# A hybrid trunk's FFN products in another order, its down contraction over both PSUM pools, and its last gate steps spread over a projection

## The chip, the core and the metric

The kernel runs on one core of one Trainium2 chip. The time is the device time of the whole program in microseconds (us), the median of several runs. Before the change it is 2257.92 us (three runs, 2255.95 to 2261.97).

The core has a matmul engine (PE, or TensorE), whose weight loads run beside its matmuls (PEld), a vector engine (DVE), an activation engine (ACT), GpSimd (POOL) and a sync engine (SP) that only issues transfers. Each engine runs its own queue of instructions in order and waits for the others by semaphores. Matmuls write to PSUM, eight banks of 128 x 512 float32; everything else lies in SBUF or in the chip's memory.

## The reference, cut to what matters

Two layers, 512 tokens, width 1024, FFN width 2816. Each layer is

```python
x = x + 0.5 * swiglu(rmsnorm(x, ffn1_norm[l]), ffn1_w_gate[l], ffn1_w_up[l], ffn1_w_down[l])
x = x + hybrid_mixer(rmsnorm(x, mix_norm[l]), w_in[l], w_out[l], ...)
x = x + 0.5 * swiglu(rmsnorm(x, ffn2_norm[l]), ffn2_w_gate[l], ffn2_w_up[l], ffn2_w_down[l])

def swiglu(h, wg, wu, wd):
    return (jax.nn.silu(h @ wg) * (h @ wu)) @ wd
```

The mixer projects its input once (`w_in`), runs an mLSTM, a Mamba-2 scan and a convolution module on the parts, and projects back (`w_out`). Two of those parts matter here: the gates (the columns `i_pre`, `f_pre` and `dt`, from which come cumulative sums, running maxima and exponentials) and `z`, a plain projection of 1024 columns under a SiLU.

## The kernel before, in words

**Precision.** A float32 product is made of three matmuls: each operand is split into a rounded high part and the rest (high x high, high x low, low x high). Weights arrive by DMA in tiles called `raw` (three buffers) or `half` (six buffers); `split_w` makes `whi` on ACT (L176) and then `wlo` on DVE (L177), each in three buffers, for 1024 columns' worth at a time. A split waits until one of its three buffers has been read for the last time by PE.

**The FFN.** There are four (two a layer), each of one block of 256 columns and five blocks of 512. A block of 512 (`gated`) computes gate and up columns together by seven products instead of eight, in the manner of Strassen and Winograd: tokens, input rows and (gate, up) columns are each cut in two. On the right stand sums of weight tiles, which a DMA with `accum_op=add`, issued by POOL (`plus`, L363), makes in place; on the left stand the normed input `xh`, `xl` (products "11", "12", "22") or combinations of its quarters `chi`, `clo` that `combine` has made (products "5", "6", "7", "3"). Each product is 24 matmuls of 128x512 in two halves of 12, each half with its own `split_w`. In the order of the text of before:

- "11" takes the gate tiles `g1` into PSUM tiles A; then `plus` adds an up tile to `g1`, while `u1` and `u2` are loaded and `plus` adds to `u1`
- "12" takes `g2` (a `raw` tile) into A; the gate's SiLU (L388) reads A
- "5" takes the changed `g1` into C; `plus` adds to `g1` again
- "6" takes that `g1` into B; `plus` adds a third time; L398 and L399 fold B and C into `u` and `w`
- "7" takes `u1` into E; L404 folds it into `w`
- "3" takes `u2` into C on top of "5"
- "22" takes the `g1` of three sums into E on top of "7"

Every use of `g1` but the first follows the landing of a `plus` transfer, which itself waits until the split of the use before has read `g1`. Then 16 transposes (L421) turn the result, and the block's down product (`contraction`, L190 to L192) adds it to the residual `xT` in eight tiles of 12 matmuls, which DVE evicts one by one (L328). The blocks overlap: block n+1's "11" runs before block n's contraction, so the order on PE is products of n, "11" of n+1, contraction of n, products of n+1. In the first FFN's first block, called the opening block below, `combine` runs on DVE and ACT at the same time, and its scratch takes four of the six `half` buffers.

**PSUM.** Two pools of four banks: `pacc` (A, C, E, projections, the contraction) and `pmix` (B, transposes, small things). A holds two `pacc` banks over the contraction, which goes round the other two.

**The mixer.** `gates` is a generator of six steps. Step 3 ends in a store of rows to memory (`ssd_rows`, L600), which POOL loads back (L720), masks (L721) and ACT exponentiates (L724). Step 4 transposes (L607, L608), takes running maxima on DVE (L609 to L618, one chunk after the other) and exponentials on ACT (L616 to L625). Step 5 transposes those (L629, L631). `weave` runs one step of one generator per step of another, so the program's text lays gate steps between the convolution and the SSD projections.

**Order.** The text order is not the order on the engines. Tile, the scheduling layer, places instructions by priority and its own cost model; `shifted(-SOON)` raises the priority of an eviction.

Of the kernel before, what the change touches and what calls it, by code (L numbers as in the profile page):

```python
# [8 lines left out]

# [2 lines left out]

# [13 lines left out]
P = 128  # L28
# [17 lines left out]
SOON = 200  # L46
# [3 lines left out]
def trunk(ctx: ExitStack, tc: tile.TileContext, I: dict, out: bass.AP):  # L50
# [26 lines left out]
    def pacc():  # L77
        return ps_p.tile([P, S], F32, tag="acc", name="pacc")
# [218 lines left out]
        for _ in contraction(acts, wrows, scale, nxt):  # L297
            pass

    def contraction(acts, wrows, scale, nxt):  # L300

        nk = len(acts)
        per = 2048 // nk // (2 * P) * 2 * P
        step = 1024 // nk // P * P
        for o in range(0, D, per):
            v = stream([w[:, o:o + per].rearrange("(k p) d -> p k d", p=P) for w in wrows], nk, per)
            for q in range(0, per, step):
                hv, lv = split_w(v[:, :, q:q + step])
                tiles = [[(hv[:, k, m * P:(m + 1) * P], lv[:, k, m * P:(m + 1) * P], *acts[k]) for k in range(nk)]
                         for m in range(step // P)]  # L310
                pss = []
                if o + q == 0:
                    pss = [pacc() for _ in tiles[0:2]]
                    for part in (slice(0, max(nk - 2, 1)), slice(max(nk - 2, 1), nk)):
                        for ps, terms in zip(pss, tiles):
                            mm3(ps, terms[part], part.start == 0, part.stop == nk)
                for m, terms in enumerate(tiles):
                    d = (o + q) // P + m
                    if m < len(pss):
                        ps = pss[m]  # L320
                    else:
                        ps = pacc()
                        mm3(ps, terms)
                    with shifted(-SOON):
                        if scale == 1.0:
                            nc.vector.tensor_tensor(xT[d], ps, xT[d], op=add)
                        else:
                            nc.vector.scalar_tensor_tensor(xT[d], ps, scale, xT[d], op0=mul, op1=add)  # L328
                    if nxt is not None:
                        nxt.prep(d)  # L330
                    if d % 2:
                        yield

    def gated(nrm, wg, wu, c0, acts):
# [5 lines left out]
        def product(left, right, ps, start=True):  # L340
            for _ in product_halves(left, right, ps, start):
                pass
# [38 lines left out]
            for t in two:  # L381
                nc.scalar.copy(u[t], A[t])
        yield
        product("12", g2, A, start=False)
        gate = [tmp() for _ in two]
        with shifted(-SOON):
            for t in two:
                nc.scalar.activation(gate[t], A[t], AF.Silu, scale=r[:, t:t + 1])  # L388
        C = [pacc() for _ in two]
        product("5", g1, C)  # L390
        plus(g1, du2)
        B = [pmix() for _ in two]
        product("6", g1, B)
        plus(g1, dg2)
        w = [tmp() for _ in two]
        with shifted(-SOON):
            for t in two:
                nc.vector.tensor_tensor(u[t], B[t], u[t], op=add)  # L398
                nc.vector.tensor_tensor(w[t], C[t], u[t], op=add)  # L399
        E = [pacc() for _ in two]  # L400
        product("7", u1, E)
        with shifted(-SOON):
            for t in two:
                nc.vector.tensor_tensor(w[t], E[t], w[t], op=add)  # L404
        product("3", u2, C, start=False)
        act = [tmp() for _ in two] + w
        with shifted(-SOON):
# [19 lines left out]
    def ffn(nrm, wg, wu, wd, nxt, side=iter(()), pair=None, ready=(), final=None):  # L427
# [7 lines left out]
        for gi in range(len(blocks) + 1):  # L435
# [36 lines left out]
            if last and final:  # L472
                final.finish(acts, wd[f0:f0 + len(acts) * P, :], sign)
            else:
                held = contraction(acts, [wd[f0:f0 + len(acts) * P, :]], sign, after)
                if gi == len(blocks) - 1 and not final:
                    next(held)
                    next(held)
# [15 lines left out]
    def mixer(l, nrm, par, nxt):  # L494
# [521 lines left out]
        weave(glu_pair(0, R), spread(gate, (0, 1, 0, 1)), 1)  # L1016
        with shifted(0):
            nrm.apply()
        weave(ssd_proj(0, G[0]), gate, 1)
        drain(z_proj(0))  # L1020
        weave(ssd_inner(0, G[0], Z[0], r01), ssd_proj(1, G[1]), 1)
        weave(ssd_inner(1, G[1], Z[0], r01), chain(glu_pair(1), ssd_proj(2, G[2]), z_proj(1)), 2)
        weave(ssd_inner(2, G[2], Z[1], r23),
# [235 lines left out]
```

## Time and profile before

| | |
|---|---|
| median of three runs | 2257.92 us |
| the profiled execution's own time | 2266.93 us |
| its span, first to last instruction | 2264.9 us |
| PE busy | 2229.0 us, 98% |
| PEld, DVE, ACT, POOL busy | 81%, 73%, 50%, 12% |
| mean granted clock of PE | 0.995 |
| read from memory | 304.65 MB, 135 GB/s |

The profile is of one execution, a little slower than the median run. "Busy" of PE is a sum over rows whose ends are modelled: matmuls overlap, a row lasts longer than the distance to the next start, so short delays between matmuls show no idle time. A row of the timeline gives start, length, engine, line, operation and the tiles (out<-in), then in brackets the idle time ahead of it and what ended it.

### The profile page before, as it was taken

How to read it: one execution, taken by the hardware profiler on the slowest of the kernel's cores; microseconds unless marked ns; L12 is line 12 of the kernel's file. 1: busy time of each engine (PE TensorE's matmuls, PEld its weight loads, DVE VectorE, ACT ScalarE, POOL GpSimd, SP SyncE). 2: the span in 40 equal slices, each digit the busy share in tenths (PEclk: the TensorE clock that was granted, in tenths of full speed). 3: DMA queues.
4: the chain of work that ended last, by engine and by line, in shares of the span. 5: the costliest groups of instructions: out<-in, count | busy, mean ns of one | idle time of the engine just before them, and what ended most of it. 6: DMA issues, size and time to landing. Idle time of an engine off the chain costs nothing.

```text
span 2264.9 us, 27297 instructions
## 1 busy us (share of the span) xinstructions
PE 2229.0 (98%) x10339; PEld 1836.5 (81%) x10339; DVE 1644.2 (73%) x2357; ACT 1126.9 (50%) x1633; POOL 274.5 (12%) x305
## 2 busy tenths in 40 slices
PE   8899999999999999999999999999999999999998
PEld 7688788788888878888887888877888888888887
DVE  6666567999966775666776666688999588666557
ACT  5443345767555543434443344466665555433334
POOL 0221110100100012111011111101101000211110
PEclk9999999999999999999999999999999999999999
DMA  6876653333332277677376777433323324867662
GB/s 200 211 186 159 158 113 95 113 94 93 107 106 72 84 198 175 171 177 175 91 185 168 168 185 168 94 96 94 111 81 108 100 68 145 201 162 167 150 155 66
DMA packets 189539, 308.62 MB, mean 136 GB/s; under 512 B 9144, under 2 KB 68952, under 8 KB 189408
## 3 DMA queue, kind: packets, MB, share of 16 engines
q1 hardware_dynamic: 139712, 208.68, 28.0%
q0 software_dynamic: 48608, 97.04, 24.3%
q8 instruction: 82, 1.34, 0.2%
q10 hardware_dynamic: 1088, 1.16, 0.1%
q14 instruction: 49, 0.40, 0.1%
HBM read 304.65 MB, written 2.19 MB: 135 GB/s over the span
## 4 chain that ended last, share of the span: by engine, by line
PE 82%; issue 6%; DMA 4%; DVE 4%; ACT 3%; POOL 1%; SPq 0%; POOLq 0%; ACTq 0%; DVEq 0%
PE pacc L191 13%; PE pacc L192 13%; PE pacc L190 13%; PE pacc L356 8%; PE pacc L357 8%; PE pacc L355 8%; DMA half<-in_ffn_w_up_dram 3%; PE pacc L880 2%; PE pacc L881 2%; PE pacc L882 2%; PE pmix L356 2%; PE pmix L357 1%; PE pmix L355 1%; DVE wlo L177 1%; PE pmix L421 1%
## 5 line engine op out<-in xcount | busy, mean ns | idle before, releaser
L176 ACT CAST whi<-raw 128x1024 fp32r<-128x1024 f32 (+1 forms) x276 | 285.8, 1037 | 415.1 <-PE pacc L191 314.0
L177 DVE TENSOR_TENSOR wlo<-half,whi 128x1024 fp32r<-128x1024 f32 x240 | 291.3, 1223 | 214.6 <-ACT whi L176 214.2
L176 ACT CAST whi<-half 128x1024 fp32r<-128x1024 f32 x240 | 250.3, 1052 | 386.2 <-PE pacc L357 162.6
L177 DVE TENSOR_TENSOR wlo<-raw,whi 128x1024 fp32r<-128x1024 f32 (+1 forms) x276 | 332.8, 1208 | 109.4 <-ACT whi L176 108.3
L190 PE MATMUL pacc<-atile,whi 128*128 128x512 f32 x928 | 361.6, 392 | 1.4 <-DVE xT L328 1.4
L191 PE MATMUL pacc<-atile,whi 128*128 128x512 f32 x928 | 362.1, 390 | 0.3
L192 PE MATMUL pacc<-atile,wlo 128*128 128x512 f32 x928 | 361.9, 390 | 0.0
L363 POOL DMA_DIRECT2D half<-in_ffn_w_up_dram x120 | 144.4, 1239 | 1077.0 <-DVE wlo L177 700.5
L328 DVE SCALAR_TENSOR_TENSOR xT<-pacc,xT 128x512 f32<-128x512 f32 x184 | 126.7, 691 | 174.8 <-PE pacc L192 174.7
L190 PE MATMUL pacc<-xh,whi 128*128 128x512 f32 x608 | 242.7, 400 | 0.0
L192 PE MATMUL pacc<-xh,wlo 128*128 128x512 f32 x608 | 237.9, 392 | 0.0
L191 PE MATMUL pacc<-xl,whi 128*128 128x512 f32 x608 | 237.7, 392 | 0.0
L190 PEld LDWEIGHTS pacc<-atile,whi 128*128 128x128 f32 x928 | 174.0, 188 | 39.0 <-DVE xT L328 3.0
L191 PEld LDWEIGHTS pacc<-atile,whi 128*128 128x128 f32 x928 | 174.2, 188 | 37.2 <-DVE atile L183 1.6
L192 PEld LDWEIGHTS pacc<-atile,wlo 128*128 128x128 f32 x928 | 174.4, 188 | 36.1
L355 PE MATMUL pacc<-whi,chi 128*128 128x512 f32 x480 | 187.4, 391 | 3.6 <-ACT whi L176 2.5
L356 PE MATMUL pacc<-wlo,chi 128*128 128x512 f32 x480 | 187.6, 391 | 0.5 <-DVE wlo L177 0.5
L355 PE MATMUL pacc<-whi,xh 128*128 128x512 f32 x480 | 188.1, 392 | 0.0
L357 PE MATMUL pacc<-whi,clo 128*128 128x512 f32 x480 | 187.4, 391 | 0.0
L356 PE MATMUL pacc<-wlo,xh 128*128 128x512 f32 x480 | 187.2, 390 | 0.0
L357 PE MATMUL pacc<-whi,xl 128*128 128x512 f32 x480 | 187.2, 390 | 0.0
L693 DVE SCALAR_TENSOR_TENSOR cacc<-upad,pA,cacc 128x512 f32<-128x512 f32 x240 | 175.8, 766 | 1.1
(330 smaller groups left out, 3727.0 us busy)
## 6 DMA issues: line engine op xcount, KB each, us to landing
half<-in_ffn_w_up_dram POOLq DMA_DIRECT2D x120, 512.0 KB, 7.0
raw<-in_ffn_w_down_dram SPq DMA_DIRECT2D x44, 1024.0 KB, 5.1
half<-in_ffn_w_up_dram SPq DMA_DIRECT2D x80, 512.0 KB, 4.6
raw<-in_w_in_dram SPq DMA_DIRECT2D x40, 1024.0 KB, 5.4
raw<-in_ffn_w_gate_dram SPq DMA_DIRECT2D x23, 1024.0 KB, 5.2
half<-in_ffn_w_gate_dram SPq DMA_DIRECT2D x40, 512.0 KB, 7.0
half<-in_ffn_w_gate_dram POOLq DMA_DIRECT2D x40, 512.0 KB, 6.0
raw<-in_w_out_dram SPq DMA_DIRECT2D x10, 1024.0 KB, 4.9
```

What stands on the lines that cost most here:

```text
L176: nc.scalar.copy(hv, v)
L177: nc.vector.tensor_tensor(lv, v, hv.bitcast(F32), op=sub)
L190: nc.tensor.matmul(ps, wh, ah, start=start and k == 0, stop=False)
L191: nc.tensor.matmul(ps, wh, al, start=False, stop=False)
L192: nc.tensor.matmul(ps, wl, ah, start=False, stop=stop and k == n - 1)
L328: nc.vector.scalar_tensor_tensor(xT[d], ps, scale, xT[d], op0=mul, op1=add)
L355: nc.tensor.matmul(ps[t], ah, hv[:, i, :], start=start and k == 0, stop=False, **more)
L356: nc.tensor.matmul(ps[t], ah, lv[:, i, :], start=False, stop=False, **more)
L357: nc.tensor.matmul(ps[t], al, hv[:, i, :], start=False, stop=k == 3, **more)
L363: nc.gpsimd.dma_start(v, b[:, 2 * j:2 * j + 2, :], accum_op=add)
L693: nc.vector.scalar_tensor_tensor(o, u[:, j:j + S], col(cA, j * 4 + c), o, op0=mul, op1=add)
L880: nc.tensor.matmul(pv[c], xh[k][:, cs(c)], hv[:, k2, :], start=k == 0, stop=False)
```

## The change

It does three things. In `gated` the order becomes "11", "5", "7", "6", "12", "3", "22"; E moves to `pmix`, so that all four `pmix` banks and four `pacc` banks are held in a block, and the three evictions into `u` and `w` come in one group. `contraction` takes its tiles' banks in turn from a list of pools, for the FFN `pacc` and `pmix`, elsewhere `pacc` alone. In the mixer, z's projection follows the first SSD projection in one chain, and the gate's last three steps are laid at the first, third and sixth step of that chain.

```diff
-    def contraction(acts, wrows, scale, nxt):
-
+    def contraction(acts, wrows, scale, nxt, banks=(pacc,)):
+
+        turn = cycle(banks)
+        bank = lambda: next(turn)()
...
-                    pss = [pacc() for _ in tiles[0:2]]
+                    pss = [bank() for _ in tiles[0:2]]
...
-                        ps = pacc()
+                        ps = bank()
...
-        product("12", g2, A, start=False)
-        gate = [tmp() for _ in two]
-        with shifted(-SOON):
-            for t in two:
-                nc.scalar.activation(gate[t], A[t], AF.Silu, scale=r[:, t:t + 1])
         C = [pacc() for _ in two]
         product("5", g1, C)
         plus(g1, du2)
+        E = [pmix() for _ in two]
+        product("7", u1, E)
         B = [pmix() for _ in two]
         product("6", g1, B)
         plus(g1, dg2)
...
                 nc.vector.tensor_tensor(u[t], B[t], u[t], op=add)
                 nc.vector.tensor_tensor(w[t], C[t], u[t], op=add)
-        E = [pacc() for _ in two]
-        product("7", u1, E)
+                nc.vector.tensor_tensor(w[t], E[t], w[t], op=add)
+        product("12", g2, A, start=False)
+        gate = [tmp() for _ in two]
         with shifted(-SOON):
             for t in two:
-                nc.vector.tensor_tensor(w[t], E[t], w[t], op=add)
+                nc.scalar.activation(gate[t], A[t], AF.Silu, scale=r[:, t:t + 1])
         product("3", u2, C, start=False)
...
-                held = contraction(acts, [wd[f0:f0 + len(acts) * P, :]], sign, after)
+                held = contraction(acts, [wd[f0:f0 + len(acts) * P, :]], sign, after, (pacc, pmix))
...
-        weave(ssd_proj(0, G[0]), gate, 1)
-        drain(z_proj(0))
+        weave(chain(ssd_proj(0, G[0]), z_proj(0)), spread(gate, (1, 0, 1, 0, 0, 1)), 1)
+        drain(gate)
```

The matmuls are the same in number and size; what moves is their order. Three places show it.

**Place one, a regular block (the first FFN's second block).** On ACT the splits name the tile that they read: `raw_859` is "12"'s `g2`, `half_797` and `half_799` are `g1`, `half_875` and `half_877` are `u1`, `half_881` and `half_883` are `u2`. Before:

```order
L176 CAST whi_1033<-raw_859 128x1024
L176 CAST whi_1037<-raw_859 128x1024
L176 CAST whi_1071<-half_797 128x1024
L176 CAST whi_1075<-half_799 128x1024
L388 ACTIVATE tmp_1065<-pacc_801,nr_321 128x512
L388 ACTIVATE tmp_1066<-pacc_802,nr_321 128x512
L176 CAST whi_1107<-half_797 128x1024
L176 CAST whi_1111<-half_799 128x1024
L176 CAST whi_1149<-half_875 128x1024
L176 CAST whi_1153<-half_877 128x1024
```

After:

```order
L176 CAST whi_1035<-half_797 128x1024
L176 CAST whi_1039<-half_799 128x1024
L176 CAST whi_1071<-half_875 128x1024
L176 CAST whi_1075<-half_877 128x1024
L176 CAST whi_1105<-half_797 128x1024
L176 CAST whi_1109<-half_799 128x1024
L176 CAST whi_1147<-raw_859 128x1024
L176 CAST whi_1151<-raw_859 128x1024
```

Two splits of `u1` now stand between the two uses of `g1`, and those of `g2` after both. On DVE, behind the same block's "6", the evictions now stand in one group ahead of the low split of "3" (`half_881`). After:

```order
L177 TENSOR_TENSOR wlo_1152<-raw_859,whi_1151 128x1024
L397 TENSOR_TENSOR u_885<-pmix_1103,u_885 128x512
L397 TENSOR_TENSOR u_886<-pmix_1104,u_886 128x512
L398 TENSOR_TENSOR tmp_1139<-pacc_1033,u_885 128x512
L398 TENSOR_TENSOR tmp_1140<-pacc_1034,u_886 128x512
L399 TENSOR_TENSOR tmp_1139<-pmix_1069,tmp_1139 128x512
L399 TENSOR_TENSOR tmp_1140<-pmix_1070,tmp_1140 128x512
L177 TENSOR_TENSOR wlo_1184<-half_881,whi_1183 128x1024
```

Before, four evictions (there L398 and L399) stood ahead of that split and the two of E (there L404) behind the next.

**Place two, the first layer's gates.** On ACT, L724 exponentiates a mask row loaded back from memory (`rb`), L616 to L625 are the gates' exponentials, `raw_3366` and `raw_3424` hold z's weights. Before:

```order
L647 ACTIVATE mtile_3191<-mtile_3191 128x512
L724 ACT_TABLE_LOAD
L724 ACTIVATE rb_3490<-rb_3490,nlc_2860 128x128
L647 ACT_TABLE_LOAD
L647 ACTIVATE mtile_3232<-mtile_3232 128x512
L616 ACT_TABLE_LOAD
L616 ACTIVATE atile_3241<-atile_3240,mc_2868 4x128 x2
L620 ACTIVATE mc_2868<-mc_2868 4x1
L176 CAST whi_3396<-raw_3366 128x1024
L616 ACTIVATE atile_3241<-atile_3240,mc_2868 4x128
L620 ACTIVATE mc_2868<-mc_2868 4x1
L625 ACTIVATE atile_3238<-atile_3238,mc_2868 4x128 x3
```

After:

```order
L176 CAST whi_3382<-raw_3352 128x1024
L644 ACTIVATE mtile_3269<-pacc_3244,pC_1811,pB_1351 128x512
L647 ACTIVATE mtile_3232<-mtile_3232 128x512
L724 ACT_TABLE_LOAD
L724 ACTIVATE rb_3490<-rb_3490,nlc_2860 128x128 x4
L724 ACTIVATE rb_3499<-rb_3499,nlc_2860 128x128 x4
L647 ACT_TABLE_LOAD
L647 ACTIVATE mtile_3269<-mtile_3269 128x512
L616 ACT_TABLE_LOAD
L616 ACTIVATE atile_3278<-atile_3277,mc_2868 4x128 x2
L176 CAST whi_3426<-raw_3424 128x1024
L620 ACTIVATE mc_2868<-mc_2868 4x1
```

Eight mask exponentials instead of one now stand ahead of the first L616, and z's second split (`whi_3382` after, `whi_3396` before) ahead of them. On PE, the transposes of step 5 (L629, L631) among z's matmuls (L880 to L882), before:

```order
L882 MATMUL pacc_3363<-whi_3368,xl0_100 128x512
L629 MATMUL pmix_3313<-ident_75,atile_3238 128x4
L880 MATMUL pacc_3362<-whi_3368,xh1_93 128x512
L629 MATMUL pmix_3313<-ident_75,atile_3238 128x4
L881 MATMUL pacc_3362<-wlo_3369,xh1_93 128x512
L882 MATMUL pacc_3362<-whi_3368,xl1_101 128x512
L629 MATMUL pmix_3313<-ident_75,atile_3238 128x4
```

After:

```order
L880 MATMUL pacc_3350<-whi_3382,xh3_95 128x512
L881 MATMUL pacc_3350<-wlo_3383,xh3_95 128x512
L882 MATMUL pacc_3350<-whi_3382,xl3_103 128x512
L629 MATMUL pmix_3410<-ident_75,atile_3275 128x4 x3
L631 MATMUL pmix_3410<-ident_75,atile_3276 128x4 x4
L880 MATMUL pacc_3348<-whi_3426,xh4_96 128x512
```

The transposes now stand together. Between the last transpose of step 4 (L608) and the first L629 stood 51 matmuls of 128x512 (45 of a projection, 6 of z) and now stand 60 (24 and 36); L607 itself stands 21 matmuls later. On DVE the low split of z's second tile now stands ahead of L609, and that of its third tile ahead of L621. The same holds in the second layer.

**Place three, the opening block on POOL.** `half_387` and `half_389` are `g1`, `half_481` and `half_483` are `u1`. Before:

```order
L363 DMA half_387<-in_ffn1_w_up_dram 128x2x512
L363 DMA half_389<-in_ffn1_w_up_dram 128x2x512
L363 DMA half_387<-in_ffn1_w_gate_dram 128x2x512
L363 DMA half_481<-in_ffn1_w_up_dram 128x2x512
L363 DMA half_483<-in_ffn1_w_up_dram 128x2x512
L363 DMA half_389<-in_ffn1_w_gate_dram 128x2x512
```

After:

```order
L365 DMA half_387<-in_ffn1_w_up_dram 128x2x512
L365 DMA half_389<-in_ffn1_w_up_dram 128x2x512
L365 DMA half_481<-in_ffn1_w_up_dram 128x2x512
L365 DMA half_483<-in_ffn1_w_up_dram 128x2x512
L365 DMA half_387<-in_ffn1_w_gate_dram 128x2x512
L365 DMA half_389<-in_ffn1_w_gate_dram 128x2x512
```

`u1`'s two sums go ahead of the third sum of `g1`. On PE the 24 matmuls of "12", which before were mixed among the opening block's contraction and stood ahead of "5", now follow "6".

## Rows read from the trace of the kernel before

**Rows 1.** The page, part 1: engine, busy us, share, instructions

```profile
PE 2229.0 (98%) x10339; PEld 1836.5 (81%) x10339; DVE 1644.2 (73%) x2357; ACT 1126.9 (50%) x1633; POOL 274.5 (12%) x305
```

**Rows 2.** The page, part 4: the chain that ended last, by engine

```profile
PE 82%; issue 6%; DMA 4%; DVE 4%; ACT 3%; POOL 1%; SPq 0%; POOLq 0%; ACTq 0%; DVEq 0%
```

**Rows 3.** Waits of PE: waiter, releaser, us in total, times, longest

```profile
PE pmix L629 <- ACT atile L625: 5.4, 2, 3.2
PE pmix L356 <- DVE wlo L177: 4.6, 7, 0.8
...
PE pmix L744 <- DVE mtile L862: 2.4, 2, 1.2
PE pacc L190 <- DVE xT L328: 1.4, 1, 1.4
```

**Rows 4.** Timeline of PE, "6" in the second FFN's first block

```profile
841.69 0.39 PE L357 MATMUL pacc<-whi,clo 128*128 128x512 f32 x1
841.92 0.39 PE L355 MATMUL pmix<-whi,chi 128*128 128x512 f32 x1
843.03 0.50 PE L356 MATMUL pmix<-wlo,chi 128*128 128x512 f32 x1 [0.72 <-DVE wlo L177]
```

**Rows 5.** Timeline of POOL, ACT and DVE, the same block

```profile
834.76 1.18 POOL L363 DMA_DIRECT2D half<-in_ffn_w_up_dram  x1 [17.89 <-DVE wlo L177]
...
840.67 1.05 ACT L176 CAST whi<-half 128x1024 fp32r<-128x1024 f32 x1 [3.30 <-DMA half<-in_ffn_w_up_dram]
...
841.75 1.23 DVE L177 TENSOR_TENSOR wlo<-half,whi 128x1024 fp32r<-128x1024 f32 x1 [5.48 <-ACT whi L176]
...
848.10 1.28 DVE L398 TENSOR_TENSOR u<-pmix,u 128x512 f32<-128x512 f32 x2
```

**Rows 6.** Groups by line, PE: xcount, busy us, mean ns, idle

```profile
L356 PE MATMUL pmix<-wlo,chi 128*128 128x512 f32 x160 | 64.9, 405 | 4.6 <-DVE wlo L177 4.6
```

**Rows 7.** Timeline of PE, the gates' last transposes, second layer

```profile
1540.47 0.26 PE L629 MATMUL pmix<-ident,atile 4*128 4x4 f32 x1 [3.21 <-ACT atile L625]
...
1543.52 0.63 PE L881 MATMUL pacc<-wlo,xh 128*128 128x512 f32 x1
```

**Rows 8.** Timeline of ACT, the same place

```profile
1534.16 0.40 ACT L724 ACTIVATE rb<-rb,nlc 128x128 f32<-128x128 f32 x1 [5.22 <-POOL rb L721]
...
1540.03 0.97 ACT L625 ACTIVATE atile<-atile,mc 4x128 f32<-4x128 f32 x3
...
1541.84 0.63 ACT L622 ACTIVATE atile<-atile 4x512 f32<-4x512 f32 x1
```

**Rows 9.** Timeline of DVE, the same place

```profile
1527.18 0.67 DVE L609 COPY atile<-pmix 4x512 f32<-4x512 f32 x1
...
1536.29 0.51 DVE L618 TENSOR_TENSOR mc<-atile,mc 4x1 f32<-4x1 f32 x1
```

**Rows 10.** Busy time by stretch; the last columns: granted clock, DMA share, GB/s

```profile
423.00:432.00 9.00, 6.79 (x25) 4.44 (x24) 7.19 (x15) 6.91 (x16) 0.00 (x0) 0.81 0.38 118
432.00:805.00 373.00, 371.07 (x1830) 311.65 (x1829) 315.10 (x518) 227.11 (x387) 23.15 (x40) 1.00 0.31 97
...
1536.00:1548.00 12.00, 8.79 (x28) 5.75 (x26) 8.16 (x15) 8.47 (x17) 1.96 (x2) 0.72 0.31 89
```

**Rows 11.** Timeline of SP, DVE and PE, the opening block

```profile
53.46 17.76 SPq L165 DMA_DIRECT2D half<-in_ffn_w_up_dram  x4
...
69.60 1.22 DVE L275 TENSOR_TENSOR clo<-half,chi 128x1024 fp32r<-128x1024 f32 x1
...
77.98 0.73 PE L355 MATMUL pacc<-whi,chi 128*128 128x512 f32 x2 [2.46 <-ACT whi L176]
...
91.42 0.39 PE L355 MATMUL pacc<-whi,xh 128*128 128x512 f32 x1
```

**Rows 12.** The page, part 6: transfers, KB, us from issue to landing

```profile
half<-in_ffn_w_up_dram POOLq DMA_DIRECT2D x120, 512.0 KB, 7.0
...
half<-in_ffn_w_up_dram SPq DMA_DIRECT2D x80, 512.0 KB, 4.6
```

More of the change, by code (lines that the diff above doesn't have):

```diff
@@ L12 @@
-from itertools import chain
+from itertools import chain, cycle
 from contextlib import ExitStack, contextmanager
```

## The prediction, on record before the result

> **What bounds the kernel now.** I read the page first: PE is busy for 98% of the span, DVE for 73%, ACT for 50% [rows 1], and the chain that ended last runs on PE for 82% [rows 2]. The other 18% of that chain are no list of delays. It passes through transfers and splits beside which PE had other work, and the waits of PE name DMA nowhere near that often. The time is that of PE's matmuls, and a change that leaves their number alone can only give back what PE loses between them. In the timeline two matmuls start 0.23 us apart while a row shows 0.39 [rows 4]: a wait shorter than 0.16 shows no idle time, and each idle time shown is 0.16 short of the delay.
>
> So I read PE's waits for the places, and the stretches for the clock. Three kinds of delay lie where the change acts. First, "6": 7 shown waits of 4.6 us together on its low split [rows 3]. Second, the gates' transposes L629: 5.4 us in two waits [rows 3], and around them the granted clock falls, to a mean of 0.81 over 9 us in the first layer and 0.72 over 12 us in the second, where the stretch between has 1.00 [rows 10]. [...] Third, the opening block: 2.46 us of waiting ahead of "5" [rows 11].
>
> **The products in another order: "6".** Why "6" is late stands in one block's timeline. POOL issues the sum into `g1` at 834.76, when the split of "5" has read it. ACT waits for the landing until 840.67, then takes 1.05; DVE's low split begins at 841.75 and takes 1.23 [rows 5]. PE wants it at 842.3 and gets it at 843.03 [rows 4]. With "7" between "5" and "6", PE has 24 matmuls more, 24 x 0.23 = 5.5 us, against a lateness that is at most 0.8 + 0.16 = 1.0. What "7" needs, `u1`, is loaded and added to well ahead in such a block, since before it stood only one product later, behind "6". What goes: 4.6 us shown, 7 x 0.16 = 1.1 hidden under rows, and delays too short to show at all, seen in L356's mean of 405 ns against 390 for an undelayed row, 160 x 0.015 = 2.4 [rows 3, 4, 6]. That is 8.1 at most and 0 if the delay only moves to another product. A part of it belongs to the opening block, which I cost apart. I take **7**.
>
> "5" now comes right after the contraction, without "12" between. The first sum into `g1` then has the contraction's 48 matmuls in an FFN's first block (11.0 us) and 96 otherwise (22 us) as cover, against a sum of 7.0 [rows 12] and splits of 2.3. Nothing gained or lost. For "22" two products stand between it and "6", as before.
>
> **Evictions in one group.** Six now stand on DVE ahead of the low split of "3", where before there were four (place one of the change). They are done one per 0.64 us or so (two end within 1.28 [rows 5]), some 3.8 us after "6" ends, and the split takes 1.23, so it ends 5.1 us after "6". Meanwhile PE runs "12", 5.5 us, and the second term of "3" wants the low part 0.2 later. Some 0.6 us of slack: cost 0, its bound above is rival C.
>
> **Banks.** The contraction's tiles now go round four banks and more instead of two. PE showed one wait there in the whole run, 1.4 us, in the opening block [rows 3]; so there is nothing to gain elsewhere. With B and E both in `pmix`, the contraction's `pmix` tiles need the eviction of B and E, which ends long before "3" and "22" do. Cost 0; its bound is rival D.
>
> **The gates.** Before, the two places cost the waits, 5.4, and 2 x 0.16 hidden, and the clock 9 x 0.19 = 1.7 and 12 x 0.28 = 3.4 [rows 3, 10]: 10.8 together. After, in the second layer, PE reaches L607 21 matmuls later, 4.8 us, and L629 nine more, 2.1. Without its wait L629 was due before at 1540.47 - 3.21 - 0.16 = 1537.1 [rows 7], so now at 1544.0. Who is late? DVE copies L607's result 4.8 us later than 1527.18, at about 1532, and in the new order the low split of z's second tile (1.2) stands ahead of it, which waits for one of the three buffers: 1533.2. From the copy to the last L618 were 9.6 us (1527.18 to 1536.80 [rows 9]): 1542.8. ACT's last exponentials (0.97 [rows 8]) then end at 1543.8, as PE comes. Of the eight mask exponentials that now stand ahead of ACT's first L616, the first was at 1534.16, held by POOL [rows 8]; eight of 0.4 and the table loads around them end near 1540, before DVE gives the last maximum, so they don't decide. L631 follows the four L629 and needs L622, behind a further low split (1.23) and short operations on DVE (about 1.4) and then 0.63 on ACT [rows 8]: 1542.8 + 1.23 + 1.4 + 0.63 = 1546.1, against PE's arrival at 1544.4. So a wait of some **1.7** stays there, now for L631 and no longer for L629. The same order holds in the first layer, and I take the same.
>
> Does the clock fall at 1.7? A wait of 1.2, twice at L744 [rows 3], left the stretch that holds the first of them at 1.00 [rows 10]; the waits of 3.2 and 2.2 (5.4 less 3.2) at L629 did not [rows 3]. I take no fall, being nearer to 1.2; 3.4 remain of 10.8, a gain of **7.4**. The ends are 3 (waits as long as the first layer's now, with its clock) and 10.8. The eight table loads fewer on ACT cost and gain nothing on PE, since ACT is half idle.
>
> **The opening block.** Here combine's scratch holds four `half` buffers, so `u1` is loaded late: SP's issue waits from 53.46 [rows 11]. "12" no longer fills PE ahead of "5", and "7" wants `u1` one product sooner. Load 4.6 and sum 7.0 [rows 12], with some 2 us for the second of a pair, put `u1` at about 67, split at 69.5. "5" ends at about 66, or 71.3 if the combinations end no earlier than the last one before, at 70.8 [rows 11]. "7" then ends near 75; "6", "12" and "3" are 72 matmuls, 16.4 us; the third sum into `g1`, issued near 75 and some 9 in landing and splitting in time, is covered. "22" starts at 91.4, where it did (91.42 [rows 11]): cost **0**. The filler that is lost ahead comes back behind. Ends: a gain of 2 (the wait of 2.46 gone), a loss of 3, and rival B.
>
> **Sum.** 7 + 7.4 = 14.4. The profiled execution took 2266.93, its span of 2264.9 and 2.0 around it; less 14.4 it is 2252.5. It stands 9.0 above the median of the runs, 2257.92; none of the terms is of that kind, so the median goes down by the same: **2243.5**.
>
> **Rivals.**
> A. The gates keep waits long enough for the clock to fall in both layers. For it: DVE and ACT do as much there as before, only moved; against: PE arrives 4.8 + 2.1 = 6.9 us later at a place where it waited 3.2. It gives back about 2 x 1.7 [rows 10] and some of the wait: 2247.5.
>
> [...]
>
> B. The opening block pays for the lost filler. `u1` lands later than I reckon, since the load, two sums and combine's scratch share one span of buffers, PE waits twice and its clock falls. Its idle there now is 2.46, and what a late `u1` could add is a product and a half of filler, 5.5 + 2.7, with 0.8 of clock: 9. 2252.5. For it: place three, where `u1`'s sums now stand ahead; against: in the sum above "7" and "22" are on time.
>
> C, on the other side. The low split of "3" comes late behind the six evictions in each of the 20 blocks of 512. It decides from 0.6 us on, which is my slack: 2 us more of DVE work in the group and PE waits 1.4 a block, 28 us, 2271. For it: DVE is 73% busy, and two rows of other work laid between would do; against: the evictions are raised in priority, and the order of place one has none between.
>
> D. Each contraction waits for a `pmix` bank and gets one stretch at the lower clock, 1.7 us [rows 10]. 20 x 1.7 = 34 over the forecast: 2278. [...]
>
> E. Better: the opening block's wait of 2.46 [rows 11] and the short ones around it go as well, with the low clock after them: 7 less, 2236.5.
>
> **How the numbers follow.** Forecast 0.56 (its own range 2239 to 2248), A 0.14, B 0.14, C 0.07, D 0.02, E 0.07. From 2234 to 2254 lie the forecast, A, B and E, 0.91 less what their own widths leave out; the bounds of "6" (0 to 8.1) and the gates (3 to 10.8) lie inside as well, save both at their worst. This kernel's measurement tells about 0.3%, 6.8 us: faster means under 2251.1. The forecast, A and E make 0.77, of which I take 0.02 off for tails: 0.75. B is within the bound, with those tails 0.17 together with a small C; slower 0.08.
>
> **What would show it.** In PE's waits no low split ahead of L356. At L629 none, at L631 two of about 1.7 behind ACT's L622, and a granted clock near 1.00 around both. "22" of the opening block at 91. No wait of "3" for its low split, no wait of L190 for an eviction. The prediction is wrong if the gain at "6" reappears as waits at L355 for whi in "3" or "5", or if the opening block grows.

## The result, and the profile after

The changed kernel takes 2244.65 us in the median (four runs, 2243.82 to 2245.71) against 2256.93 for the kernel before on the same chip: a ratio of 0.9942, 95% interval 0.9924 to 0.9959. Run again later it was 0.9933 (0.9921 to 0.9946). Two executions of the kernel before, beside e13, took 3184 and 8139 us at granted clocks of 0.66 and 0.27, and no ratio or range below has them. The prediction was 2243.5, between 2234 and 2254.

The page of the changed kernel, part 1 and part 4 (the answers to [rows 1, 2]):

```profile
PE 2216.3 (99%) x10339; PEld 1836.9 (82%) x10339; DVE 1638.5 (73%) x2357; ACT 1117.8 (50%) x1625; POOL 275.1 (12%) x305
PE 95%; DVE 2%; ACT 1%; DMA 1%; issue 1%; POOL 0%; SPq 0%; POOLq 0%; ACTq 0%
```

The chain that ended last now runs on PE for 95% instead of 82%. The waits of PE, as in [rows 3] (waiter, releaser, us in total, times, longest):

```profile
PE pacc L357 <- ACT chi L274: 3.1, 2, 1.6
...
PE pmix L744 <- DVE mtile L862: 2.4, 2, 1.2
...
PE pmix L357 <- ACT whi L176: 1.4, 1, 1.4
...
PE pacc L357 <- DVE xT L330: 0.8, 1, 0.8
PE pacc L359 <- DVE clo L275: 0.8, 1, 0.8
PE pmix L358 <- DVE wlo L177: 0.8, 1, 0.8
```

L357 to L359 are L355 to L357 of before. L629 is gone, and L631 has not taken its place. Of the seven waits of a `pmix` product on its low split one is left, in the opening block; all the waits at L357 to L359 lie there too.

**"6".** POOL and PE in the second FFN's first block, the place of [rows 4, 5]:

```profile
815.59 1.18 POOL L365 DMA_DIRECT2D half<-in_ffn_w_up_dram  x1 [6.24 <-DVE wlo L177]
822.67 1.20 POOL L365 DMA_DIRECT2D half<-in_ffn_w_up_dram  x1 [5.90 <-DVE wlo L177]
```

```profile
834.08 0.39 PE L357 MATMUL pmix<-whi,chi 128*128 128x512 f32 x1
834.30 0.39 PE L358 MATMUL pmix<-wlo,chi 128*128 128x512 f32 x1
```

The first sum that "6" needs is issued 18.5 us ahead of its first matmul at 834.08, where it was 7.2 before (834.76 to 841.92). "6" goes on to its low split without a wait. That is more than the 5.5 us of "7", because the first half of "5" is now split while the contraction still runs.

**The evictions.** DVE behind that "6", and PE where "3" begins:

```profile
839.23 1.28 DVE L397 TENSOR_TENSOR u<-pmix,u 128x512 f32<-128x512 f32 x2
840.43 1.28 DVE L398 TENSOR_TENSOR tmp<-pacc,u 128x512 f32<-128x512 f32 x2
841.62 1.28 DVE L399 TENSOR_TENSOR tmp<-pmix,tmp 128x512 f32<-128x512 f32 x2
842.82 2.35 DVE L177 TENSOR_TENSOR wlo<-half,whi 128x1024 fp32r<-128x1024 f32 x2
```

```profile
844.96 0.39 PE L357 MATMUL pacc<-whi,chi 128*128 128x512 f32 x1
845.18 0.39 PE L358 MATMUL pacc<-wlo,chi 128*128 128x512 f32 x1
```

The row of 2.35 us holds the two low splits of "3". The first ends at about 844.0, PE wants it at 845.18: 1.2 us of slack, where 0.6 was reckoned.

**The gates.** DVE, ACT and PE in the first layer's gates, ACT and PE at the end of the second's, the place of [rows 7 to 9], and the stretches around both as in [rows 10]:

```profile
416.34 0.67 DVE L609 COPY atile<-pmix 4x512 f32<-4x512 f32 x1
...
425.02 0.12 DVE L618 TENSOR_TENSOR mc<-atile,mc 4x1 f32<-4x1 f32 x1
...
427.65 0.63 ACT L622 ACTIVATE atile<-atile 4x512 f32<-4x512 f32 x1 [0.69 <-DVE atile L621]
...
428.08 0.34 PE L629 MATMUL pmix<-ident,atile 4*128 4x4 f32 x3
...
428.33 0.41 PE L631 MATMUL pmix<-ident,atile 4*128 4x4 f32 x4
...
1530.43 0.63 ACT L622 ACTIVATE atile<-atile 4x512 f32<-4x512 f32 x1 [0.69 <-DVE atile L621]
...
1531.12 0.41 PE L631 MATMUL pmix<-ident,atile 4*128 4x4 f32 x4
```

```profile
418.00:430.00 12.00, 12.00 (x58) 9.76 (x57) 12.00 (x28) 10.35 (x22) 2.61 (x2) 1.00 0.26 87
1520.00:1533.00 13.00, 13.00 (x63) 10.58 (x62) 13.00 (x30) 11.21 (x26) 3.78 (x3) 1.00 0.28 89
```

L622 ends at 428.28 and 1531.06, and L631 starts at 428.33 and 1531.12: just in time. The granted clock is 1.00 where it was 0.81 and 0.72.

**The opening block** ([rows 11]), SP, POOL and PE:

```profile
53.30 12.21 SPq L165 DMA_DIRECT2D half<-in_ffn_w_up_dram  x4
58.94 1.18 POOL L365 DMA_DIRECT2D half<-in_ffn_w_up_dram  x1 [6.64 <-DVE half L273]
61.68 1.20 POOL L365 DMA_DIRECT2D half<-in_ffn_w_up_dram  x1 [1.56 <-DVE clo L275]
63.91 0.80 PE L357 MATMUL pacc<-whi,chi 128*128 128x512 f32 x1 [1.59 <-ACT chi L274]
71.09 0.50 PE L357 MATMUL pmix<-whi,chi 128*128 128x512 f32 x1 [1.42 <-ACT whi L176]
```

```profile
91.27 0.39 PE L357 MATMUL pmix<-whi,xh 128*128 128x512 f32 x1
```

"22" starts at 91.27, before at 91.42. The time is now lost ahead of pieces of "5", which wait for the combinations (`chi`), and of "7", which waits for `u1` (1.42 at 71.09), but it is as much.

**Where PE loses time.** To put all this in one measure I took the starts of PE's matmuls from each trace and added up by how much the distance of two neighbours exceeds the usual one (0.227 us after a matmul of 512 columns, 0.216 after 256, 0.11 after fewer). It counts waits, low clock and delays too short to show as waits. In us, one profiled execution each; its own time stands last:

| kernel | start | opening block | FFNs beyond it | gates | rest | own time |
|---|---|---|---|---|---|---|
| before, as in the rows above | 8.4 | 10.1 | 16.7 | 11.6 | 11.3 | 2266.93 |
| before, second profile (e4) | 8.6 | 11.1 | 12.9 | 8.9 | 10.7 | 2260.97 |
| changed | 9.4 | 10.0 | 6.5 | 0.1 | 10.3 | 2243.82 |
| changed, second profile (e12) | 7.0 | 11.1 | 7.5 | 0.1 | 10.5 | 2243.70 |

So the FFNs and the gates, two of the places that the prediction named, carry the gain: 21 to 22 us against the first profile of before and 14 to 15 against the second. The median moved by 12 to 15.

### The profile page after: what moved, and what is told of

The parts are those of the page before. It is cut to its first block, busy times and chain, and to the rows that moved or that the text cites. A ratio compares the mean times of both kernels' runs of the same rounds, so it can differ in the third digit from the quotient of the medians.

```text
span 2242.1 us, 27179 instructions
## 1 busy us (share of the span) xinstructions
PE 2216.3 (99%) x10339; PEld 1836.9 (82%) x10339; DVE 1638.5 (73%) x2357; ACT 1117.8 (50%) x1625; POOL 275.1 (12%) x305
## 4 chain that ended last, share of the span: by engine, by line
PE 95%; DVE 2%; ACT 1%; DMA 1%; issue 1%; POOL 0%; SPq 0%; POOLq 0%; ACTq 0%
PE pacc L191 11%; PE pacc L192 11%; PE pacc L190 11%; PE pacc L357 6%; PE pacc L359 6%; PE pacc L358 6%; PE pmix L358 5%; PE pmix L359 5%; PE pmix L357 5%; PE pmix L190 3%; PE pmix L191 3%; PE pmix L192 3%; PE pacc L880 3%; PE pacc L882 3%; PE pacc L881 3%; PE pmix L421 1%
## 5 line engine op out<-in xcount | busy, mean ns | idle before, releaser
L177 DVE TENSOR_TENSOR wlo<-raw,whi 128x1024 fp32r<-128x1024 f32 (+1 forms) x276 | 332.6, 1207 | 151.9 <-ACT whi L176 149.9
L177 DVE TENSOR_TENSOR wlo<-half,whi 128x1024 fp32r<-128x1024 f32 x240 | 291.7, 1223 | 169.2 <-ACT whi L176 169.2
L191 PE MATMUL pacc<-atile,whi 128*128 128x512 f32 x592 | 231.2, 391 | 1.0 <-DVE atile L183 1.0
L192 PE MATMUL pacc<-atile,wlo 128*128 128x512 f32 x592 | 231.2, 391 | 0.0
L190 PE MATMUL pacc<-atile,whi 128*128 128x512 f32 x592 | 230.9, 392 | 0.0
L330 DVE SCALAR_TENSOR_TENSOR xT<-pmix,xT 128x512 f32<-128x512 f32 x92 | 63.5, 690 | 109.7 <-PE pmix L192 109.6
L191 PEld LDWEIGHTS pacc<-xl,whi 128*128 128x128 f32 x608 | 114.3, 188 | 23.7 <-DVE xl L293 0.9
L192 PEld LDWEIGHTS pacc<-xh,wlo 128*128 128x128 f32 x608 | 114.1, 188 | 23.6 <-DVE wlo L177 0.7
L190 PEld LDWEIGHTS pacc<-xh,whi 128*128 128x128 f32 x608 | 114.3, 188 | 23.2
L191 PEld LDWEIGHTS pacc<-atile,whi 128*128 128x128 f32 x592 | 111.2, 188 | 25.1 <-DVE atile L183 2.3
L192 PE MATMUL pmix<-atile,wlo 128*128 128x512 f32 x336 | 130.8, 389 | 0.0
L190 PE MATMUL pmix<-atile,whi 128*128 128x512 f32 x336 | 130.8, 389 | 0.0
L191 PE MATMUL pmix<-atile,whi 128*128 128x512 f32 x336 | 130.8, 389 | 0.0
L192 PEld LDWEIGHTS pacc<-atile,wlo 128*128 128x128 f32 x592 | 111.2, 188 | 22.9
L190 PEld LDWEIGHTS pacc<-atile,whi 128*128 128x128 f32 x592 | 111.0, 188 | 22.9 <-DVE xT L330 0.3
```

The lines of the kernel that those rows point to most:

```text
L177: nc.vector.tensor_tensor(lv, v, hv.bitcast(F32), op=sub)
L190: nc.tensor.matmul(ps, wh, ah, start=start and k == 0, stop=False)
L191: nc.tensor.matmul(ps, wh, al, start=False, stop=False)
L192: nc.tensor.matmul(ps, wl, ah, start=False, stop=stop and k == n - 1)
```

## The experiments

Medians and ratios are against the kernel before on the same chip, the bracket is the 95% interval.

**e1, the gates alone.** The kernel before with

```diff
-        weave(ssd_proj(0, G[0]), gate, 1)
-        drain(z_proj(0))
+        weave(chain(ssd_proj(0, G[0]), z_proj(0)), spread(gate, (1, 0, 1, 0, 0, 1)), 1)
+        drain(gate)
```

> The kernel before with the mixer's part of the change alone (z's projection chained behind the first SSD projection, the gate's last steps spread over it). In the profiles of before and of the change the stretches around the gates lost 11.5 us to waits and half clock before and 0.0 after. Theory: the gates are half of the gain and independent of the FFN's order: no wait at L629 or L631, granted clock 1.00 around them, 5 to 8 us off the median of before (the profiled execution of before was 9 us above its median, so the profile's 11.5 is an upper end), and the waits of 6 on its low split stay. Rival one (the gates were late only because the product order before delayed nothing there; the FFN is the whole of the gain): within 2 us of before. Rival two (gates are nearly all): 11 us or more.

Measured: 2250.23 against 2258.21, 0.9970 (0.9959 to 0.9981), 8 us. The gates lose 0.1, the FFNs 15.5 as before. The theory holds; both rivals fall.

**e2, the order alone.** The changed kernel with the old text of the mixer and

```diff
-                held = contraction(acts, [wd[f0:f0 + len(acts) * P, :]], sign, after, (pacc, pmix))
+                held = contraction(acts, [wd[f0:f0 + len(acts) * P, :]], sign, after)
```

> The changed kernel with its FFN order 11, 5, 7, 6, 12, 3, 22 and E in the pmix pool, but with the contraction on pacc alone and the mixer's text as before. Theory: the gain at 6 comes from 7 standing ahead of it, not from the banks: no low split ahead of 6 among PE's waits outside the opening block, 5 to 8 us off the median of before, gates' waits at L629 as before. Rival (the contraction's banks matter as much): under 3 us, with waits of the contraction for its evictions or of 5 for the contraction's last eviction.

Measured: 2257.01 against 2258.21, 0.9993 (0.9985 to 1.0002): 1.2 us, within the noise. The theory, that the order by itself brings the gain, falls. The profiled execution took 2251.91, the fastest of twelve (the slowest took 2260.34). PE's waits, two of them in the second FFN's first contraction, and DVE there:

```profile
PE pacc L190 <- DVE xT L330: 9.7, 11, 1.8
```

```profile
815.48 0.50 PE L190 MATMUL pacc<-atile,whi 128*128 128x512 f32 x1 [0.77 <-DVE xT L330]
821.93 0.50 PE L190 MATMUL pacc<-atile,whi 128*128 128x512 f32 x1 [0.68 <-DVE xT L330]
```

```profile
813.60 1.23 DVE L177 TENSOR_TENSOR wlo<-half,whi 128x1024 fp32r<-128x1024 f32 x1 [1.37 <-ACT whi L176]
814.74 1.28 DVE L330 SCALAR_TENSOR_TENSOR xT<-pacc,xT 128x512 f32<-128x512 f32 x2
```

The low splits of 6 no longer release PE in the regular blocks, but the contraction now waits. In an FFN's first block it has six matmuls a tile, 1.4 us, on two banks; when a low split of 1.23 comes ahead of two evictions on DVE, both banks are full. Before, the scheduler had put five matmuls of "12" among this contraction, four ahead of its third tile and one ahead of its seventh, which are the two places where PE now waits. With "12" behind "6" there is nothing to put in. Six of the eleven waits, 4.9 us, lie in the three later FFNs' first contractions; the other five, 4.8 us, lie in the opening block, which in this execution loses no more than before.

**e3, the banks alone.** The kernel before with only the changes to contraction and its call:

```diff
+        turn = cycle(banks)
+        bank = lambda: next(turn)()
...
-                        ps = pacc()
+                        ps = bank()
```

> The kernel before with the contraction's tiles alternating between the two PSUM pools alone. Theory: the contraction waited for a bank once, 1.4 us, in the opening block, so this is worth 0 to 1.5 us. Rival (banks carry part of the FFN's gain by letting the contraction end sooner ahead of 5): 3 us or more. Rival on the other side (the contraction's pmix tiles wait for B's eviction or hold back B and the transposes): slower by 2 us or more.

Measured: 2253.66 against 2258.21, 0.9979 (0.9970 to 0.9988), 4.5 us: the theory (0 to 1.5) falls, and the size is as the first rival has it. With four banks the contraction is no longer mixed with "12", which then stands whole between the contraction and "5". PE's waits for 6's low split (L359 here) and POOL and PE in the second FFN's first block:

```profile
PE pmix L359 <- DVE wlo L177: 1.2, 3, 0.7
```

```profile
830.20 1.18 POOL L366 DMA_DIRECT2D half<-in_ffn_w_up_dram  x1 [16.39 <-DVE wlo L177]
838.49 0.39 PE L358 MATMUL pmix<-whi,chi 128*128 128x512 f32 x1
838.72 0.39 PE L359 MATMUL pmix<-wlo,chi 128*128 128x512 f32 x1
```

The sum that "6" needs is issued 8.3 us ahead of it instead of 7.2, and the low split is there. In the measure of the table the FFNs lose some 9 to 10 us here, between those of before and the 6.5 to 7.5 of the changed kernel.

**e4, the kernel before again**, with no edit, for a second profile.

> The kernel before, unchanged, for a second profile of it. The first profiled execution took 9 us more than the median of its runs. Theory: the extra lies in the very places that the change acts on (the gates' waits and the half clock after them, and the waits of 6), since they end on transfers whose landing varies: with an execution near 2257 those places lose some 12 us instead of 21.7. Rival: the extra lies elsewhere (start, end, other layers), and those places lose the same as in the first profile.

Measured: 2260.84 against 2258.21, 1.0010 (1.0001 to 1.0019), so that two builds of one text differ by 0.1%. Its profiled execution took 2260.97, at its median and 6 less than the first:

```profile
PE pmix L629 <- ACT atile L625: 4.7, 2, 3.2
...
PE pmix L356 <- DVE wlo L177: 3.0, 5, 0.8
```

FFNs and gates lose 21.8, not the 28.3 of the first profile, and nearly all of the difference lies in them, as the theory says. It did not reach the 12 that I expected of an execution near 2257, and no profile of one was had: what the places lose in those runs stays open.

**e13, the banks taken back alone.** The changed kernel with the diff of e2.

> The changed kernel with the contraction on the pacc pool alone, the product order and the gates as changed: the second pool taken back by itself. The order alone, with the old gates, showed eleven waits of the contraction for its evictions, 9.7 us together, which neither the kernel before nor the changed one has. Theory (with 12 no longer mixed among the first, short contraction of each FFN, two banks don't cover an eviction and four do): those waits come back, and the kernel is 4 to 8 us over the changed one, 0.9955 to 0.997 of the kernel before. Rival (the second pool gives nothing beside the new order, and the order by itself was held up by the old gates): within 2 us of the changed kernel.

Measured: 2250.68 against 2258.98, 0.9968 (0.9957 to 0.9979), 6 to 8 us over the changed kernel by the two ratios of that. The waits are back:

```profile
PE pacc L190 <- DVE xT L330: 9.3, 10, 1.8
```

The theory holds. Without the pool the kernel is where the gates alone put it (0.9970), so the order without the pool adds nothing to them. The pool without the order adds something: e3 alone has 4.5 of the 6 to 8 us that order and pool are worth together beside the gates. The gates and the pool with the old order were not run; the ratios of e1 and e3 multiplied make 0.9949, against 0.9942 and 0.9933 for the whole change, which leaves some 2 to 4 us for the order beside both, less than their intervals can tell from nothing.

**e5, "12" in the middle.** The changed kernel with

```diff
         product("5", g1, C)
         plus(g1, du2)
-        E = [pmix() for _ in two]
-        product("7", u1, E)
+        product("12", g2, A, start=False)
...
         product("6", g1, B)
         plus(g1, dg2)
...
+        E = [pacc() for _ in two]
+        product("7", u1, E)
```

> The changed kernel (banks and gates as changed) with the product order 11, 5, 12, 6, 7, 3, 22 and E back in the pacc pool: 12 instead of 7 between 5 and 6, the folds apart as in the kernel before. Theory: any product of 24 matmuls between 5 and 6 takes the wait of 6 away, so the regular blocks are as in the changed kernel; and in the opening block 12 can be mixed with 5, which waits there for the combinations, and u1 gets a product more of time, so the opening loses some 5 us where the changed kernel loses 10: 0 to 5 us under the changed kernel's 2244.7, no low split of 6 among the waits. Rival (7 has to be the product that is moved, because with 12 there the use of E, or 7 and 3, come late): 3 us or more over the changed kernel, with new waits at 7, 3 or 22.

Measured: 2245.75 against 2259.35, 0.9937 (0.9924 to 0.9949), the same as the changed kernel. "12" between "5" and "6" does what "7" does there: the FFNs lose 7.6. The hope for the opening block fell: it loses 10.6, now in one place ahead of "7", 5.0 of it in two waits:

```profile
PE pacc L357 <- ACT whi L176: 5.0, 2, 4.8
```

**e6, "12" back in front.** The changed kernel with

```diff
+        product("12", g2, A, start=False)
...
         C = [pacc() for _ in two]
         product("5", g1, C)
...
-        product("12", g2, A, start=False)
...
         product("3", u2, C, start=False)
```

> The changed kernel with 12 back in its old place: 11, 12, 5, 7, 6, 3, 22. Now 3, which adds onto C, follows 6 directly. Theory (the slack ahead of 3 is 12's 24 matmuls): its first matmul waits for the evictions that read C and for its low split behind six of them, 2.5 to 4.5 us in each of 20 blocks, 50 to 90 us over the changed kernel; and where the wait is over 2 us the granted clock falls after it. Rival (the six evictions overlap 6, or the scheduler fills in other work): under 10 us over.

Measured: 2279.11 against 2259.35, 1.0087 (1.0073 to 1.0101), slower than before and some 33 us over the changed kernel: short of the theory's 50 to 90, and far over the rival's 10. One line of PE's waits, and DVE and PE behind a "6":

```profile
PE pacc L357 <- DVE tmp L403: 29.9, 19, 1.6
```

```profile
147.60 1.28 DVE L402 TENSOR_TENSOR u<-pmix,u 128x512 f32<-128x512 f32 x2
148.79 1.28 DVE L403 TENSOR_TENSOR tmp<-pacc,u 128x512 f32<-128x512 f32 x2
149.62 0.47 PE L357 MATMUL pacc<-whi,chi 128*128 128x512 f32 x1 [1.57 <-DVE tmp L403]
```

"3" adds onto C and waits until L403 has read its half of it. The wait was there, but shorter than I expected: PE goes on after the first of the two L403, and the low split of "3" stood ahead of the evictions, not behind (the next L177 is that of its second half). Nor did the clock fall: the stretch 100 to 375, with four of these waits, has 1.00.

```profile
100.00:375.00 275.00, 268.35 (x1214) 220.56 (x1213) 171.55 (x202) 110.44 (x135) 44.51 (x48) 1.00 0.60 145
```

**e7 and e8, the gate's last step one step earlier and later.**

```diff
-spread(gate, (1, 0, 1, 0, 0, 1))
+spread(gate, (1, 0, 1, 0, 1))            # e7
+spread(gate, (1, 0, 1, 0, 0, 0, 1))      # e8
```

> The changed kernel with the gate's last step one step earlier in the chain: L629 stands 14 matmuls, 3.2 us, earlier, everything else about the gates as changed. In the changed kernel L622's result is there 0.1 us before or after PE comes for it, so there is no slack. Theory: a wait of about 3 us comes back at L629 or L631 in each layer, the granted clock falls after it, and the kernel is 6 to 9 us slower than the changed one. Rival (ACT and DVE take the gate's operations earlier when they are asked for earlier): within 2 us of the changed kernel.

> The changed kernel with the gate's last step one step later in the chain: L629 stands 36 matmuls, 8.2 us, later. Theory: nothing waits at L629 or L631 in the changed kernel, so more room gives nothing: within 2 us, unless what is read behind the last step (en, ws and the row stores) comes late for the mLSTM heads, which are far behind. Rival (timed executions without a profile do wait there, as the transfers that hold up the mask exponentials vary): 2 to 4 us faster.

Measured: e7 2247.72 and e8 2245.86 against 2259.35, 0.9946 (0.9934 to 0.9959) and 0.9941 (0.9928 to 0.9953). Against the two ratios of the changed kernel that is 1 to 3 us slower for e7 and 0 to 2 for e8, so e8 is as its theory says. e7's expectation of 6 to 9 us was wrong: the gates lose 2.7 there. The scheduler lays the transposes singly among z's matmuls there, and each waits only for its own piece. L629 in its list of waits:

```profile
PE pmix L629 <- ACT atile L625: 0.8, 2, 0.6
```

**e9 and e10, combine's scratch elsewhere.** The changed kernel (e9) and e5 (e10), with

```diff
-                t = half()
-                a5, a6, a7, a3 = [t[:, i * 256:(i + 1) * 256] for i in range(4)]
+                ts = [atile().bitcast(F32) for _ in range(2)]
+                a5, a6, a7, a3 = [ts[i // 2][:, i % 2 * 256:(i % 2 + 1) * 256] for i in range(4)]
...
-                nc.scalar.copy(hi, t)
-                nc.vector.tensor_tensor(lo, t, hi.bitcast(F32), op=sub)
+                for i, t in enumerate(ts):
+                    h = slice(i * S, i * S + S)
+                    nc.scalar.copy(hi[:, h], t)
+                    nc.vector.tensor_tensor(lo[:, h], t, hi[:, h].bitcast(F32), op=sub)
```

> The changed kernel with combine's scratch in two atile buffers a step (its rounded copy and rest then go in two pieces of 512 columns) instead of one of the six half buffers, so that u1 and u2 can be loaded in the opening block before combine is done. In the changed kernel the opening block loses 10 us: 5 waits for the combinations, 7 for u1, with a lower clock between. Theory (u1 is late because its load waits for combine's scratch): POOL issues u1's sums before 50 instead of 58.9 and 61.7, the waits ahead of 7 are gone, and the opening loses 3 to 6: 4 to 7 us under the changed kernel on the same chip. Rival (the transfers themselves are the limit in this stretch, DMA share 0.85, or combine is): within 2 us of it, with u1's whi or the combinations as late as before.

> The order 11, 5, 12, 6, 7, 3, 22 with banks and gates as changed, and combine's scratch in atile buffers. With the scratch in half buffers this order lost as much in the opening block as the changed one, in one place: 4.8 us ahead of 7 for u1, and the lower clock after it. Theory: with u1 early and 12 mixed with 5 while the combinations are made, the opening loses 2 to 4 us: 6 to 8 under the changed kernel on the same chip. Rival (transfers or combine are the limit): within 2 us of it.

**e12, the changed kernel again**, on the same chip as e9 and e10, with no edit.

> The changed kernel unchanged, on the same chip as the two others. Theory and rival agree: 0.994 of the kernel before, between 0.992 and 0.996.

Measured, against 2258.50: e9 2237.15, 0.9902 (0.9888 to 0.9915); e10 2236.52, 0.9899 (0.9884 to 0.9914); e12 2243.70, 0.9933 (0.9921 to 0.9946). Both are some 7 us faster than the changed kernel, as their theories have it. In e9 POOL issues `u1`'s two sums one behind the other from 21.01, as soon as the first load has landed (58.94 and 61.68 in the changed kernel), and PE waits twice in the block:

```profile
21.01 2.53 POOL L367 DMA_DIRECT2D half<-in_ffn_w_up_dram  x2 [16.56 <-DMA half<-in_ffn_w_up_dram]
```

```profile
52.52 0.50 PE L359 MATMUL pmix<-whi,chi 128*128 128x512 f32 x1 [1.08 <-ACT whi L176]
62.83 0.50 PE L359 MATMUL pacc<-whi,chi 128*128 128x512 f32 x1 [0.95 <-ACT chi L276]
```

With `u1` there, the scheduler mixes "7" with "5", and of the waits for the combinations one of 0.95 is left. The opening block loses 3.0 in e9 and 1.7 in e10, after 11.1 in e12. The scratch was the limit, not the transfers. The edit also makes the rounded copies and rests in two pieces; what that adds by itself was not run.

## Why the prediction was right, and where not

The time came out 1.2 us from the forecast. The terms of the gates, the opening block and the evictions stand by themselves; the step on the banks was wrong, which makes the size of "6" luck in part, and the choice of frame hides how the sum was made up.

**"6", 7 us.** The FFNs lose 7 to 8 us less on average over the profiles (14.8 to 7.0), as the term has it. The mechanism holds in its first half: with a product between, the low split is on time, and e5 shows that it need not be "7". But the order by itself gains nothing clear of the noise (e2), and the pool by itself takes the FFNs to some 9 to 10 already (e3). So some 3 of the 7 to 8 come with the order, the rest with the pool. That order and pool together make the 7 that was put down for the order is luck.

**Banks, 0: this step was wrong.** I read from one wait of 1.4 us that two banks were enough, and priced the second pool at nothing. Two banks were enough because matmuls of "12" stood in the short contractions, and the same change takes "12" away. Without the pool, contractions wait for 9 to 10 us (e2, e13), about half of it in the opening block, and the kernel is 6 to 8 us slower (e13); with the pool alone, 4.5 us are gained (e3). The sum came out because I charged nothing for the lost filler there either: the pool pays for it. That is the cover whose loss I had costed only in the opening block.

**Gates, 7.4.** e1 measured 8 (4 to 9 by its interval), with the waits of [rows 7] gone and a granted clock of 1.00 from 418 to 432 us and from 1520 to 1535 us, where [rows 10] have 0.81 and 0.72. The 1.7 that I left at L631 isn't there. I had put L609 10.8 us ahead of PE's arrival at L629, and it was 11.7 ahead (416.34 to 428.08); from L609 to the last L618 I took the 9.6 of before, and it was 8.8 (to 425.14); the way on to L622's end was 3.1 instead of 3.3. The three make 1.9, as much as the wait. Whether the clock would have stayed up after a wait of 1.7, as the step on it took, was not put to the test; in e3 the 14 us around one of 1.4 at the same place have a mean of 0.88.

**Opening block, 0; evictions, 0.** Both hold: 10.1 and 11.1 before, 10.0 and 11.1 after, "7" and "22" near the forecast times, `u1`'s load held by combine's scratch as said (e9 shows it by taking that away). The slack of "3" is 1.2.

**The frame.** I subtracted 14.4 from an execution 9 us above the median, and from the median alike. By the profiles that execution lost 22 us more than the changed kernel, so part of its 9 us lay in the very terms of the sum; e4's lost 16 more. Had I priced gates and "6" exactly from the first profile, 21 to 22, the forecast for the median would have been too low. The waits left at L631 (3.4) and the cut from 8.1 to 7 made up for most of that: the sum is nearer than its parts, and that too is luck.

**The rivals.** None came. C is near something real, which e6 shows: as soon as "12" no longer stands between "6" and "3", PE waits 1.57 us a block and the kernel loses 33 us. But there PE waits for the eviction of C, not for the low split that C named. D's stretch at a lower clock in each contraction did not show: with nothing but the banks changed (e3) the mean granted clock is 0.995, as before, and in the changed kernel the later blocks of the first FFN, from 100 to 375 us, have 1.00, as they had before.

## What to carry to other kernels

A resource that shows no wait may be covered by filler that the change moves: when a product is taken out of a place, ask what it was covering there, and price that with the resource. Where the text order is scheduled, look at the mixing of both products in the new order before calling a term zero. And look for who holds the buffer that a late load waits for: moving four scratch tiles gave some 7 us more, half of what the whole change gave.

## What the runs showed of the hardware

The clock after a wait doesn't follow from the length of the wait alone. The first layer's wait at L629 was 2.2 us in the kernel before and the clock fell (0.81 over 9 us [rows 10]); in e2 it was 2.2 as well, and the clock stayed at 1.00; in e3 the 14 us around one of 1.4 have a mean of 0.88. In e6 the stretch 100 to 375, with four waits of 1.57, has 1.00, while in e1 the 12 us around two waits at a "6" in the second layer's first FFN, 0.93 and 0.76 with 1.3 us from one to the other, have a mean of 0.86. The stretches with the gates of e2 and e3, first layer, and the two waits of e1 and the stretch around them:

```profile
410.00:424.00 14.00, 11.79 (x53) 8.84 (x52) 13.22 (x26) 10.24 (x19) 4.72 (x6) 1.00 0.42 129
```

```profile
418.00:432.00 14.00, 12.61 (x51) 9.07 (x50) 12.81 (x24) 11.22 (x21) 2.53 (x2) 0.88 0.25 76
```

```profile
1183.56 0.50 PE L355 MATMUL pmix<-whi,chi 128*128 128x512 f32 x1 [0.93 <-ACT whi L176]
1184.82 0.55 PE L356 MATMUL pmix<-wlo,chi 128*128 128x512 f32 x1 [0.76 <-DVE wlo L177]
```

```profile
1180.00:1192.00 12.00, 10.31 (x37) 7.81 (x36) 5.27 (x5) 4.11 (x5) 2.39 (x2) 0.86 0.70 112
```

What decides it was not tried. Executions of one kernel differ too: 2254 to 2264 us for the kernel before, 2242 to 2246 for the changed one, which has fewer such waits. The two profiles of the kernel before differ by 6 us: the FFNs and the gates lose 28.3 in the first and 21.8 in the second, and around the first layer's gates the second has a granted clock of 1.00 (418 to 432 us) where the first has 0.81 [rows 10]. For the other executions that is not shown.
